# Gate and up products in seven half-width products, output products placed between them, and another order of the recurrent blocks

## The chip, the cores and the metric

The kernel runs on one core of a Trainium2 chip. The number to judge is the device time of one execution in microseconds (us). Five engines of the core appear in the profile: PE (TensorE; its weight loads are shown apart as PEld), DVE (VectorE), ACT (ScalarE), POOL (GpSimd) and SP (SyncE, which here only issues transfers). The engines run side by side, and each works through its own instructions in a fixed order.

## The reference, cut to what matters

Two models follow each other on one sequence of 512 tokens with 1024 features, all in float32. The first has two recurrent blocks (attention, a linear recurrence and a convolution side by side). The second has two layers, each with a mixer, a cross attention and a gated feed-forward part:

```
D_FF = 2816

def swiglu(h, w_gate_up, w_down):
    g, u = jnp.split(h @ w_gate_up, 2, axis=-1)
    return (jax.nn.silu(g) * u) @ w_down

    for l in range(DEPTH):                       # first_block, DEPTH = 2
        h = rms_norm(x, norm_g[l])
        proj = h @ w_in[l]
        ...
    for i in range(DEPTH):                       # second_block
        ...
        x = x + swiglu(rms_norm_2(x, g_ffn[i]), w_gate_up[i], w_down[i])
    return rms_norm_2(x, g_final)
```

## The kernel before, in words

Everything is kept feature-major: `X` is eight tiles of 128 features x 512 tokens. A float32 number is split into a rounded high part and a low part (`hl`, `split`), and each product of two numbers is made of three matmuls (`mm3`): high x high, high x low, low x high.

Weights come in chunks of eight 128x128 blocks (512 KB) in the order in which they are used (`weights`). For a chunk SP issues a load into `wr`, ACT casts it to the high part `wh`, and DVE (or POOL, below) subtracts to get the low part `wl`. `wr`, `wh` and `wl` share six buffers of one pool tag `w`, taken in turn, so that two chunks are in flight. `dense_tile` makes one output tile of 128 features x 512 tokens in one PSUM bank: for eight blocks that is 24 matmuls of 512 columns.

The feed-forward part (`ffn`) has 22 tiles of hidden features, in four groups of 6, 6, 5 and 5 (`FG`). A hidden tile takes two dense tiles, gate and up, from one chunk each; DVE and ACT make silu(gate) x up from them, and `hl` splits the result. The output products of a group (`dn`, eight tiles, each followed by an addition to `X` on DVE) come after the gate and up products of the next group. The last group's output products follow at the end, in the first layer under the next stage's settings, in the second in `finish`, which works in halves of 256 tokens: the same three matmuls with 256 columns.

The recurrent blocks (`block1`, run twice) mix generators, each yielding after a step, in the order of two hand-written strings. In them U is the recurrence's input, G the convolution's input, K the compressed keys, Z, N and C the output gates, Q, V, M and A the attention, B and O the recurrence's tail, T the convolution's tail; V holds the products `vg` with the tokens as output rows (lines L478 to L480). A digit sets `wp`: of every four chunks so many have their low part made on POOL in place of DVE.

Tile decides the order of instructions on each engine from the program's order and the priorities that the code gives.

## Time and profile before

| what | value |
|---|---|
| median of 3 runs | 2249.3 us (2245.65 to 2253.51) |
| the profiled execution, its own time | 2249.68 us |
| its span, first to last instruction | 2247.9 us |
| first recurrent block, second | 0 to 402 us, 402 to 806 us |
| first feed-forward part, second | 1132 to 1490 us, 1857 to 2214 us |
| the last halves (`finish`) | 2214 to 2248 us |
| mean granted clock of PE | 0.986 |

The time of an execution holds a little more than the span. An engine's busy time is the union of its instructions; PE's matmuls overlap each other in it, so that a full row of PE says that it always had a matmul in flight, and the distance from one matmul's start to the next one's says how fast it goes.

### The profile page before, as it was taken

How to read it: one execution, taken by the hardware profiler on the slowest of the kernel's cores; microseconds unless marked ns; L12 is line 12 of the kernel's file. 1: busy time of each engine (PE TensorE's matmuls, PEld its weight loads, DVE VectorE, ACT ScalarE, POOL GpSimd, SP SyncE). 2: the span in 40 equal slices, each digit the busy share in tenths (PEclk: the TensorE clock that was granted, in tenths of full speed). 3: DMA queues.
4: the chain of work that ended last, by engine and by line, in shares of the span. 5: the costliest groups of instructions: out<-in, count | busy, mean ns of one | idle time of the engine just before them, and what ended most of it. 6: DMA issues, size and time to landing. Idle time of an engine off the chain costs nothing. (4 is left out here: it accounts for less than half of the span.)

```text
span 2247.9 us, 29297 instructions
## 1 busy us (share of the span) xinstructions
PE 2149.0 (96%) x11068; PEld 1717.2 (76%) x11068; DVE 1454.2 (65%) x2511; ACT 956.8 (43%) x1821; POOL 390.1 (17%) x419
## 2 busy tenths in 40 slices
PE   8999989999999999998999999999999999999998
PEld 6777867777786778666878888878767788888887
DVE  7998685599877646875565444554776556544444
ACT  4432475334247543664543222233586554322223
POOL 4533201453231151002020000010010202000002
PEclk9999999999999999999999999999999999999999
DMA  4343211233331123212333333322322233333332
GB/s 143 109 121 108 66 29 48 85 108 108 110 97 38 38 75 93 72 43 63 98 105 100 94 94 95 102 85 85 97 60 76 66 85 96 102 94 94 94 101 87
DMA packets 61436, 194.73 MB, mean 87 GB/s; under 512 B 8432, under 2 KB 10480, under 8 KB 61296
## 3 DMA queue, kind: packets, MB, share of 16 engines
q1 hardware_dynamic: 52848, 179.75, 26.9%
q10 hardware_dynamic: 8448, 13.12, 2.1%
q8 instruction: 87, 1.43, 0.3%
q14 instruction: 53, 0.43, 0.1%
HBM read 182.61 MB, written 2.10 MB: 82 GB/s over the span
## 5 line engine op out<-in xcount | busy, mean ns | idle before, releaser
L440 ACT CAST wh<-wr 128x1024 fp32r<-128x1024 f32 (+2 forms) x312 | 322.9, 1035 | 608.0 <-DMA wr<-ws 551.2
L373 DVE TENSOR_TENSOR wl<-wr,wh 128x1024 fp32r<-128x1024 f32 x240 | 297.6, 1240 | 333.1 <-PE ps_m L419 159.5
L418 PE MATMUL ps_m<-xh,wh 128*128 128x512 f32 x808 | 321.8, 398 | 13.0 <-ACT wh L440 8.5
L420 PE MATMUL ps_m<-xh,wl 128*128 128x512 f32 x808 | 319.0, 395 | 1.2 <-POOL wl L373 1.0
L419 PE MATMUL ps_m<-xl,wh 128*128 128x512 f32 x808 | 318.3, 394 | 1.7 <-DVE xl L376 1.7
L420 PE MATMUL ps_s<-xh,wl 128*128 128x512 f32 x680 | 269.7, 397 | 9.8 <-DVE wl L373 6.9
L418 PE MATMUL ps_s<-xh,wh 128*128 128x512 f32 x680 | 269.2, 396 | 2.9 <-ACT ti L385 2.2
L419 PE MATMUL ps_s<-xl,wh 128*128 128x512 f32 x680 | 267.5, 393 | 0.0
L370 POOL TENSOR_TENSOR sq<-sq 128x512 f32<-128x512 f32 (+1 forms) x56 | 78.8, 1406 | 969.0 <-ACT sq L385 969.0
L373 POOL TENSOR_TENSOR wl<-wr,wh 128x1024 fp32r<-128x1024 f32 (+2 forms) x72 | 170.9, 2373 | 403.4 <-PE ps_m L420 152.0
L418 PEld LDWEIGHTS ps_m<-xh,wh 128*128 128x128 f32 x808 | 153.0, 189 | 51.0 <-ACT wh L440 11.2
L385 ACT ACTIVATE p<-ps_s,mn 128x512 f32<-128x512 f32 (+3 forms) x288 | 165.9, 581 | 57.7 <-PE ps_t L819 21.6
L420 PEld LDWEIGHTS ps_m<-xh,wl 128*128 128x128 f32 x808 | 152.7, 189 | 34.6 <-POOL wl L373 1.7
L419 PEld LDWEIGHTS ps_m<-xl,wh 128*128 128x128 f32 x808 | 152.9, 189 | 34.2 <-DVE xl L376 3.5
L376 DVE SCALAR_TENSOR_TENSOR ps_s<-up,params,ps_s 128x512 f32<-128x512 f32 x232 | 169.7, 748 | 2.4
L826 ACT COPY ptt<-ps_t 128x512 f32<-128x512 f32 (+3 forms) x288 | 131.1, 478 | 90.8 <-PE ps_t L819 78.1
L420 PEld LDWEIGHTS ps_s<-xh,wl 128*128 128x128 f32 x680 | 129.2, 190 | 41.8 <-DVE wl L373 9.4
L418 PEld LDWEIGHTS ps_s<-xh,wh 128*128 128x128 f32 x680 | 129.4, 190 | 31.8 <-ACT ti L385 3.8
L419 PEld LDWEIGHTS ps_s<-xl,wh 128*128 128x128 f32 x680 | 129.4, 190 | 27.0
L819 PE MATMUL ps_t<-consts,p 128*128 128x128 f32 x848 | 132.8, 280 | 12.1 <-ACT ptt L826 9.6
L819 PEld LDWEIGHTS ps_t<-consts,p 128*128 128x128 f32 x848 | 97.0, 140 | 53.3 <-ACT ptt L826 24.3
L370 DVE TENSOR_TENSOR X<-ps_m,X 128x512 f32<-128x512 f32 (+1 forms) x100 | 66.4, 664 | 62.0 <-PE ps_m L420 62.0
(518 smaller groups left out, 4090.1 us busy)
## 6 DMA issues: line engine op xcount, KB each, us to landing
wr<-ws SPq DMA_DIRECT2D x318, 512.0 KB, 3.6
strip<-strips ACTq DMA_DIRECT2D x8, 480.0 KB, 3.8
wr<-ws SPq DMA_DIRECT2D x8, 384.0 KB, 3.1
X<-x SPq DMA_DIRECT2D x8, 256.0 KB, 4.9
mem<-mem SPq DMA_DIRECT2D x8, 256.0 KB, 2.7
wr<-ws SPq DMA_DIRECT2D x7, 256.0 KB, 2.8
tab<-tables SPq DMA_DIRECT2D x6, 256.0 KB, 2.7
out_dram<-ox SPq DMA_DIRECT2D x8, 128.0 KB, 1.7
```

The costliest lines, as they stand in the source:

```text
L370: (eng or self.nc.vector).tensor_tensor(out=out, in0=a, in1=b, op=ALU.add)
L373: (eng or self.nc.vector).tensor_tensor(out=out, in0=a, in1=b, op=ALU.subtract)
L376: self.nc.vector.scalar_tensor_tensor(out=out, in0=a, scalar=s, in1=b, op0=op0, op1=op1)
L385: return self.nc.scalar.activation(out, in_, func, **k)
L418: mm(out, ah, bh, start=first, stop=False)
L419: mm(out, ah, bl, start=False, stop=False)
L420: return mm(out, al, bh, start=False, stop=last)
L440: nc.scalar.copy(wh[:, :n], wr[:, :n])
L819: nc.tensor.transpose(t[:, j * P:(j + 1) * P], p[:, j * P:(j + 1) * P], self.con("ident"))
L826: nc.scalar.copy(dst, src)
```

## The change

A hidden tile is now of kind `p` (as before) or `s`. A string, `FFN_ORDER`, gives the kinds of the 22 tiles, 5 `p` and 17 `s`, and puts 24 letters `d` between them, each one output tile of the oldest group that is waiting. For a tile `s` the pair gate and up, the two halves of the input features (even and odd tiles of `X`) and the two halves of the tokens are taken as 2x2 blocks, and the product is made with seven products of blocks and some sums in place of eight products. Each of the seven is a sum over four pairs of input tiles, of three matmuls each with 256 columns: 84 matmuls of 256 in place of 48 of 512. The sums of weights (`ws7`: `s1` to `s4`) and their splitting are made for each tile on DVE and ACT; the sums of inputs (`halves_combined`) once for each layer; the sums of products when they leave PSUM. The raw weights and their sums lie in the six buffers of the tag `pt`, the four split parts (`wah`, `wal`, `wsh`, `wsl`) in the six of `w`. Four PSUM banks, one of each of the tags m, s, t and o, are taken by a tile `s`; there are two of each.

In the recurrent blocks the letters stand in another order, the digit before the first letters is 4 in place of 3, and the 3 that began the second string ends it.

```diff
@@ -29,6 +29,8 @@
 CONV_K = 31
 CPB = 8
 FG = (6, 6, 5, 5)
+FFN_ORDER = "pppspssddsssddssddddsdsdsddddssddddpdssdsddsdd"
+KINDS = [c for c in FFN_ORDER if c in "ps"]
 
 A_ = np.arange
 
@@ -127,8 +129,14 @@
         dense(f"xo{l}", "w_xo_2", (l,), [_r(P * n, P) for n in range(8)], kt(4))
         f0 = 0
         for g, n in enumerate(FG):
-            dense(f"gu{l}{g}", "w_gate_up_2", (l,),
-                  [_r(o + P * (f0 + i), P) for i in range(n) for o in (0, FF)], kt(8))
+            for i in range(f0, f0 + n):
+                gc, uc = _r(P * i, P), _r(FF + P * i, P)
+                if KINDS[i] == "p":
+                    dense(f"gu{l}_{i}", "w_gate_up_2", (l,), [gc, uc], kt(8))
+                    continue
+                ph[f"gu{l}_{i}"] = [
+                    _blk("w_gate_up_2", (l,), _r(P * (4 * c + 2 * q + k), P), cols)
+                    for c in range(2) for k, cols in ((0, gc), (1, gc), (1, uc), (0, uc)) for q in range(2)]
             dense(f"dn{l}{g}", "w_down_2", (l,), [_r(P * m, P) for m in range(8)],
                   [_r(P * (f0 + i), P) for i in range(n)])
             f0 += n
@@ -855,8 +863,8 @@
         return done
 
 
-    FIRST = "/UUG3cUp/GGUKGkGKZZgkZGZkB/kQ|/AkOOkGkGkO/NOAAQkQAQVM"
-    SECOND = "3NTMTATACAMAAAACCCNTQTN|TQATTTMT|TATAA/ATA"
+    FIRST = "/UU4cGUpGGUKGkGKZZ/gZGkZkBkQ|AkOOkGGOk/NOAAQkkQAQVM"
+    SECOND = "NTQTATACA/NAMAACCCTTNTATQA/TTM|MATAATATTA3"
 
     def block1(self, l):
         xhl = self.norm(f"norm_g{l}")
@@ -1553,29 +1561,134 @@
         self.run_held()
         self.residual(f"xo{l}", ys)
 
+    def gate_up(self, name, xhl, _):
+        w = self.weights(name)
+        pg = self.dense_tile(w, xhl)
+        z, th, u = (self.f("d", nm) for nm in ("fg", "ft", "fu"))
+        self.stt(z, pg, 0.5, self.RB)
+        self.act(th, z, AF.Tanh)
+        self.stt(z, th, 1.0, z, op0=ALU.add)
+        pu = self.dense_tile(w, xhl)
+        self.mul(u, pu, self.RB)
+        self.mul(z, z, u)
+        return z, u
+
+    def halves_combined(self, gname):
+
+        h = T // 2
+        slots = iter([("c", T)] * 4 + [("p", T)] * 6 + [("up", 544)] * 3 + [("lup", 516)] + [("tab", T)] * 2)
+        bufs = dict(self.SLOTS, up=3, lup=1, tab=2)
+        out = []
+        for q in range(KD // 2):
+            x1, x2 = self.X[2 * q], self.X[2 * q + 1]
+            g1, g2 = self.par(gname, 2 * q), self.par(gname, 2 * q + 1)
+            ta, tb = self.f("n", "ta"), self.f("n", "tb")
+            self.sub(ta[:, :h], x1[:, h:], x1[:, :h])
+            self.act(ta[:, :h], ta[:, :h], AF.Copy, scale=g1)
+            self.stt(ta[:, h:], x2[:, h:], g2, ta[:, :h], op1=ALU.subtract)
+            self.act(tb[:, :h], x1[:, h:], AF.Copy, scale=g1)
+            self.stt(tb[:, :h], x2[:, h:], g2, tb[:, :h], op1=ALU.subtract)
+            self.stt(tb[:, h:], x2[:, :h], g2, ta[:, h:], op1=ALU.subtract)
+            ts = []
+            for t in (ta, tb):
+                parts = []
+                for nm in ("th", "tl"):
+                    tag, n = next(slots)
+                    parts.append(self.sp.tile([P, n], F32R, name=nm, tag=tag, bufs=bufs[tag])[:, :T])
+                self.split(*parts, t)
+                ts += [tuple(x[:, e * h:e * h + h] for x in parts) for e in range(2)]
+            out.append(ts)
+        return out
+
+    def gate_up7(self, name, xhl, ts):
+
+
+        nc, h, q = self.nc, T // 2, 2 * P
+        px, py, pz, pv = (self.ps(t) for t in "msto")
+        p1, p2, p3, p4, p5, p7, p6 = px[:, :h], px[:, h:], py[:, :h], py[:, h:], pz[:, :h], pz[:, h:], pv[:, :h]
+        ends = (p2, p3, p7, p6)
+        begun = {}
+
+        def product(out, bank, w, o, b, first, last):
+            a = tuple(x[:, o:o + P] for x in w)
+            if first and bank in begun:
+                with self.tc.issue_after(begun[bank].ins):
+                    self.mm3(out, a, b, False, last)
+            else:
+                m = nc.tensor.matmul(out, a[0], b[0], start=first, stop=False)
+                if first:
+                    begun[bank] = m
+                nc.tensor.matmul(out, a[0], b[1], start=False, stop=False)
+                nc.tensor.matmul(out, a[1], b[0], start=False, stop=last)
+
+        for c in range(2):
+            self.nchunk += 1
+            with self.tc.high_priority(offset=self.WPRI):
+                wr, sm = (self.pt(nm, [P, CPB * P], F32) for nm in ("wr7", "ws7"))
+                nc.sync.dma_start(out=wr, in_=self.ap["ws"][CHUNK0[name] + c])
+                wah, wal, wsh, wsl = (self.sp.tile([P, CPB * P], F32R, name=nm, tag="w", bufs=self.NW["w"])
+                                      for nm in ("wah", "wal", "wsh", "wsl"))
+                a11, a12, a22, a21 = (wr[:, k * q:k * q + q] for k in range(4))
+                s1, s2, s3, s4 = (sm[:, k * q:k * q + q] for k in range(4))
+                nc.scalar.copy(wah[:, :3 * q], wr[:, :3 * q])
+                self.sub(wal[:, :3 * q], wr[:, :3 * q], wah[:, :3 * q].bitcast(F32))
+                self.add(s1, a21, a22)
+                self.sub(s2, s1, a11)
+                self.sub(s3, a11, a21)
+                self.sub(s4, a12, s2)
+                nc.scalar.copy(wsh, sm)
+                self.sub(wsl, sm, wsh.bitcast(F32))
+            for w, todo in (((wah, wal), ((p1, 0, 0), (p2, 0, 1), (p4, 1, 2))),
+                            ((wsh, wsl), ((p3, 1, 3), (p5, 2, 0), (p6, 3, 1), (p7, 2, 2)))):
+                for e in range(2):
+                    k = 2 * c + e
+                    x1, x2 = xhl[2 * k], xhl[2 * k + 1]
+                    t1, t2, t3, t4 = ts[k]
+                    lo, hi = (lambda x: tuple(y[:, :h] for y in x)), (lambda x: tuple(y[:, h:] for y in x))
+                    rhs = (lo(x1), lo(x2), t4) if w[0] is wah else (hi(x2), t1, t2, t3)
+                    for (out, bank, o), b in zip(todo, rhs):
+                        product(out, bank, w, o * q + e * P, b, k == 0, k == KD // 2 - 1 and out in ends)
+        s, u34 = self.f("n", "u2"), self.f("n", "u34")
+        z, th, u = (self.f("d", nm) for nm in ("fg", "ft", "fu"))
+        nc.scalar.copy(s[:, :h], p1)
+        self.add(z[:, :h], p2, s[:, :h])
+        self.add(s[:, h:], p6, s[:, :h])
+        pair = lambda x: x.rearrange("p (a n) -> p a n", a=2)
+        self.add(pair(u34), pair(pz), s[:, h:].unsqueeze(1).to_broadcast([P, 2, h]))
+        self.add(z[:, h:], p3, u34[:, :h])
+        self.stt(z, z, 0.5, self.RB)
+        self.act(th, z, AF.Tanh)
+        self.add(u[:, :h], p4, u34[:, h:])
+        self.add(u[:, h:], p5, u34[:, h:])
+        self.mul(u, u, self.RB)
+        self.stt(z, th, 1.0, z, op0=ALU.add)
+        self.mul(z, z, u)
+        return z, u
+
     def ffn(self, l, out=None):
         xhl = self.norm(f"g_ffn_2{l}")
         hid = [None] * len(FG)
 
-        def gu(g):
-            w = self.weights(f"gu{l}{g}")
-            hs = []
-            for i in range(FG[g]):
-                pg = self.dense_tile(w, xhl)
-                z, th, u = (self.f("d", nm) for nm in ("fg", "ft", "fu"))
-                self.stt(z, pg, 0.5, self.RB)
-                self.act(th, z, AF.Tanh)
-                self.stt(z, th, 1.0, z, op0=ALU.add)
-                pu = self.dense_tile(w, xhl)
-                self.mul(u, pu, self.RB)
-                self.mul(z, z, u)
-                hs.append(self.hl("a" if i % 2 else "z", z, "hid"))
-            hid[g] = hs
-
-        gu(0)
-        for g in range(1, len(FG)):
-            gu(g)
-            self.residual(f"dn{l}{g - 1}", hid[g - 1])
+        ts = []
+        todo, n = [], 0
+        for ch in FFN_ORDER:
+            if ch == "d":
+                if todo and next(todo[0], "end") == "end":
+                    todo.pop(0)
+                continue
+            if ch == "s" and not ts:
+                ts += self.halves_combined(f"g_ffn_2{l}")
+            g = next(g for g in range(len(FG)) if n < sum(FG[:g + 1]))
+            z, u = (self.gate_up if ch == "p" else self.gate_up7)(f"gu{l}_{n}", xhl, ts)
+            if hid[g] is None:
+                hid[g] = []
+            hid[g].append(self.hl("a" if len(hid[g]) % 2 else "z", z, "hid"))
+            n += 1
+            if n == sum(FG[:g + 1]) and g < len(FG) - 1:
+                todo.append(self.residual_tiles(f"dn{l}{g}", hid[g]))
+        for t in todo:
+            for _ in t:
+                pass
         name = f"dn{l}{len(FG) - 1}"
         if out is None:
             self.enter("c")
```

The lines of the changed kernel's helpers are numbered 8 higher than before (L418 to L420 of `mm3` are L426 to L428, L373 is L381); L1618 to L1622 are the three matmuls in `product`.

The order of instructions shows what moves where. On PE, in the middle of the first feed-forward part (`ps_` with a letter is the PSUM tile by its tag, `xh` and `xl` the split input, `wh` and `wl` a chunk's split weights), before:

```order
L418 MATMUL ps_s_11208<-xh_10502,wh_11211 128x512
L419 MATMUL ps_s_11208<-xl_10503,wh_11211 128x512
L420 MATMUL ps_s_11208<-xh_10502,wl_11212 128x512
L418 MATMUL ps_s_11208<-xh_10506,wh_11211 128x512
L419 MATMUL ps_s_11208<-xl_10507,wh_11211 128x512
L420 MATMUL ps_s_11208<-xh_10506,wl_11212 128x512
```

and in a tile `s` of the changed kernel (`th` and `tl` are the split sums of inputs, `wsh` and `wsl` those of weights):

```order
L1618 MATMUL ps_s_11181<-xh_10494,wsh_11189 128x256
L1621 MATMUL ps_s_11181<-xl_10495,wsh_11189 128x256
L1622 MATMUL ps_s_11181<-xh_10494,wsl_11190 128x256
L1618 MATMUL ps_t_11182<-th_10788,wsh_11189 128x256
L1621 MATMUL ps_t_11182<-tl_10789,wsh_11189 128x256
L1622 MATMUL ps_t_11182<-th_10788,wsl_11190 128x256
L1618 MATMUL ps_o_11183<-th_10788,wsh_11189 128x256
L1621 MATMUL ps_o_11183<-tl_10789,wsh_11189 128x256
L1622 MATMUL ps_o_11183<-th_10788,wsl_11190 128x256
```

Every matmul has half as many columns and its own weights, and the products of three banks alternate.

On DVE, in the first feed-forward part (`fg` and `fu` are the gate and up tile on their way to the hidden tile, `rb` the norm's factor), the whole work of one hidden tile before:

```order
L373 TENSOR_TENSOR wl_11064<-wr_11061,wh_11063 128x1024
L376 SCALAR_TENSOR_TENSOR fg_11017<-ps_s_10986,rb_10566 128x512
L376 SCALAR_TENSOR_TENSOR fg_11017<-ft_11018,fg_11017 128x512
L373 TENSOR_TENSOR wl_11101<-wr_11098,wh_11100 128x1024
L367 TENSOR_TENSOR fu_11019<-ps_m_11023,rb_10566 128x512
L367 TENSOR_TENSOR fg_11017<-fg_11017,fu_11019 128x512
L373 TENSOR_TENSOR hidl_11057<-fg_11017,hidh_11056 128x512
```

and twelve of the 21 kinds of row that a tile `s` has, where tiles `s` follow each other:

```order
L378 TENSOR_TENSOR u34_11490<-ps_t_11373,u2_11489 128x512
L381 TENSOR_TENSOR wsl_11520<-ws7_11515,wsh_11519 128x1024
L378 TENSOR_TENSOR fg_11491<-ps_s_11372,u34_11490 128x256
L378 TENSOR_TENSOR ws7_11711<-wr7_11710 128x256
L381 TENSOR_TENSOR ws7_11711<-wr7_11710 128x256
L384 SCALAR_TENSOR_TENSOR fg_11491<-fg_11491,rb_10566 128x512
L381 TENSOR_TENSOR wal_11575<-wr7_11571,wah_11574 128x768
L381 TENSOR_TENSOR ws7_11711<-ws7_11711,wr7_11710 128x256
L378 TENSOR_TENSOR fu_11493<-ps_s_11372,u34_11490 128x256
L378 TENSOR_TENSOR fu_11493<-ps_t_11373,u34_11490 128x256
L384 SCALAR_TENSOR_TENSOR fg_11491<-ft_11492,fg_11491 128x512
L381 TENSOR_TENSOR ws7_11711<-wr7_11710,ws7_11711 128x256
```

The rows of one tile's results are mixed with the weights of the tiles behind it: `wsl_11520` belongs to the next tile, `ws7_11711` to the one after it.

On POOL, around the products `vg` of the first recurrent block (`qo` is a query tile's rotation), before:

```order
L370 TENSOR_TENSOR qo_1580<-qo_1580,rs__1582 128x512
L373 TENSOR_TENSOR wl_1771<-wr_1768,wh_1770 128x768
L370 TENSOR_TENSOR qo_1625<-qo_1625,rs__1627 128x512
L373 TENSOR_TENSOR wl_1801<-wr_1798,wh_1800 128x768
L370 TENSOR_TENSOR qo_1717<-qo_1717,rs__1719 128x512
L373 TENSOR_TENSOR wl_1831<-wr_1828,wh_1830 128x768
L373 TENSOR_TENSOR wl_2191<-wr_2188,wh_2190 128x1024
```

and in the changed kernel:

```order
L378 TENSOR_TENSOR qo_1608<-qo_1608,rs__1610 128x512
L381 TENSOR_TENSOR wl_1741<-wr_1738,wh_1740 128x768
L381 TENSOR_TENSOR wl_1771<-wr_1768,wh_1770 128x768
L381 TENSOR_TENSOR wl_1801<-wr_1798,wh_1800 128x768
L378 TENSOR_TENSOR qo_1717<-qo_1717,rs__1719 128x512
L381 TENSOR_TENSOR wl_1831<-wr_1828,wh_1830 128x768
L381 TENSOR_TENSOR wl_1972<-wr_1969,wh_1971 128x1024
```

All four chunks of `vg` are on POOL now, where the first of them (`wl_1741`) was on DVE before. Over the whole program POOL makes 98 low parts in place of 72.

## Rows read from the trace of the kernel before

**Rows 1.** The page's first part: busy time, share of the span, instructions.

```profile
PE 2149.0 (96%) x11068; PEld 1717.2 (76%) x11068; DVE 1454.2 (65%) x2511; ACT 956.8 (43%) x1821; POOL 390.1 (17%) x419
```

**Rows 2.** Busy time by stage: both recurrent blocks, then both feed-forward parts.

```profile
core 0: us, PE busy (x) PEld busy (x) DVE busy (x) ACT busy (x) POOL busy (x), PEclk, DMA share, GB/s
0.00:402.00 402.00, 372.05 (x1971) 292.66 (x1972) 319.69 (x639) 179.52 (x370) 129.38 (x114) 0.98 0.30 89
402.00:806.00 404.00, 380.99 (x2036) 299.96 (x2035) 313.22 (x597) 175.46 (x366) 124.81 (x90) 0.98 0.28 83
1132.00:1490.00 358.00, 355.59 (x1559) 291.37 (x1558) 182.59 (x218) 106.13 (x128) 14.57 (x18) 1.00 0.32 96
1857.00:2214.00 357.00, 356.96 (x1600) 294.29 (x1599) 185.62 (x222) 108.66 (x132) 14.81 (x19) 1.00 0.34 99
```

**Rows 3.** PE's waits in the first feed-forward part: total us, times, longest.

```profile
PE ps_s L418 <- DVE X L370: 2.2, 1, 2.2
PE ps_s L420 <- DVE wl L373: 0.2, 1, 0.2
```

**Rows 4.** Timeline of PE, second feed-forward part: a bank's first matmul (start, duration).

```profile
2030.97 0.40 PE L418 MATMUL ps_m<-hidh,wh 128*128 128x512 f32 x1
...
2035.19 0.39 PE L418 MATMUL ps_s<-xh,wh 128*128 128x512 f32 x1
...
2040.65 0.39 PE L418 MATMUL ps_m<-xh,wh 128*128 128x512 f32 x1
...
2046.09 0.39 PE L418 MATMUL ps_s<-xh,wh 128*128 128x512 f32 x1
```

**Rows 5.** Timeline of PE in `finish`: matmuls of 256 columns, 15 to a bank.

```profile
2214.77 0.28 PE L418 MATMUL ps_s<-hidh,wh 128*128 128x256 f32 x1
...
2220.05 0.28 PE L418 MATMUL ps_m<-hidh,wkh 128*128 128x256 f32 x1
...
2221.37 0.28 PE L420 MATMUL ps_m<-hidh,wkl 128*128 128x256 f32 x1
```

**Rows 6.** Groups of PEld in `finish`, 2214 to 2225: count, busy, mean ns.

```profile
L418 PEld LDWEIGHTS ps_s<-hidh,wh 128*128 128x128 f32 x10 | 1.9, 188 | 0.0
```

**Rows 7.** Groups of DVE by shape: feed-forward part 1200 to 1400, then 256-wide, whole run.

```profile
L373 DVE TENSOR_TENSOR wl<-wr,wh 128x1024 fp32r<-128x1024 f32 x37 | 45.3, 1225 | 70.1 <-PE ps_m L419 35.0 <-PE ps_s L419 31.6 <-ACT wh L440 3.5
L373 DVE TENSOR_TENSOR hidl<-fg,hidh 128x512 fp32r<-128x512 f32 x13 | 9.0, 693 | 11.1 <-ACT hidh L403 11.1
...
L370 DVE TENSOR_TENSOR X<-ps_m,X 128x256 f32<-128x256 f32 x8 | 3.4, 424 | 5.1 <-PE ps_m L420 5.1
```

**Rows 8.** Timeline of DVE, first feed-forward part: rows that follow each other directly.

```profile
1265.08 1.23 DVE L373 TENSOR_TENSOR wl<-wr,wh 128x1024 fp32r<-128x1024 f32 x1 [2.22 <-PE ps_m L419]
1266.22 0.68 DVE L367 TENSOR_TENSOR fu<-ps_m,rb 128x512 f32<-128x512 f32 x1
1266.94 0.69 DVE L367 TENSOR_TENSOR fg<-fg,fu 128x512 f32<-128x512 f32 x1
```

**Rows 9.** Groups of ACT by shape: feed-forward part 1200 to 1400, then `finish`.

```profile
L440 ACT CAST wh<-wr 128x1024 fp32r<-128x1024 f32 x36 | 37.8, 1050 | 83.1 <-DMA wr<-ws 83.1
L403 ACT CAST hidh<-fg 128x512 fp32r<-128x512 f32 x13 | 8.1, 620 | 33.2 <-DVE fg L367 27.4 <-PE ps_m L419 5.8
...
L548 ACT COPY rb<-ps_o 128x256 f32<-128x256 f32 x2 | 0.7, 372 | 5.9 <-PE ps_o L530 5.9
```

**Rows 10.** The page's sixth part: transfers, KB each, us to landing.

```profile
wr<-ws SPq DMA_DIRECT2D x318, 512.0 KB, 3.6
```

**Rows 11.** Timeline of PE in `vg`, first recurrent block: two waits for POOL.

```profile
224.56 0.40 PE L479 MATMUL ps_s<-wl,xh 128*128 128x280 f32 x1 [1.18 <-POOL wl L373]
...
229.23 0.40 PE L479 MATMUL ps_s<-wl,xh 128*128 128x280 f32 x1 [1.32 <-POOL wl L373]
```

**Rows 12.** Groups by shape in both recurrent blocks, POOL then DVE.

```profile
L373 POOL TENSOR_TENSOR wl<-wr,wh 128x1024 fp32r<-128x1024 f32 x63 | 154.1, 2446 | 388.6 <-PE ps_m L420 152.0 <-PE ps_m L419 118.1 <-ACT wh L440 52.9
...
L373 DVE TENSOR_TENSOR ql<-qo,qh 128x512 fp32r<-128x512 f32 x8 | 11.3, 1412 | 4.0 <-ACT qh L403 4.0
```

## The prediction, made before the changed kernel had run

> **What bounds the kernel now.** I read the page first, then each stage, since the page's shares are averages. PE is busy for 96% of the span, DVE for 65% [rows 1]. By stage [rows 2] the two feed-forward parts are the purest case: PE is busy in 355.6 of 358 us and in 357.0 of 357, at a full granted clock, with DVE at 183 and 186. The waits of PE in the first of them come to 2.4 us [rows 3]. So a microsecond of matmul taken out of this stage is a microsecond of the whole, as long as the other engines keep up. The recurrent blocks are different: PE is busy for 372 of 402 us and 381 of 404, DVE for 320 and 313.
>
> A busy PE does not say how fast it goes, so I read the distance between starts. A gate or up tile is 24 matmuls: from 2040.65 to 2046.09, or 0.2267 us each. An output tile of a group of six is 18: from 2030.97 to 2035.19, 0.2344 us each [rows 4]. `finish` has the same three matmuls with 256 columns: 45 of them from 2214.77 to 2220.05, 0.1173 us each, and the slowest stretch behind it has 11 from 2220.05 to 2221.37, 0.120 us each [rows 5].
>
> **The change, part by part.** *PE.* A tile `p` costs 48 x 0.2267 = 10.88 us, a tile `s` 84 x 0.1173 = 9.85 us. That is 1.03 us a tile, and with 17 tiles in each of two layers 35.0 us. Bounds: 0.120 us each leaves 0.80 us a tile, 27 us in all. If a half-width matmul on these inputs went at half of 0.2267, 84 x 0.1133 = 9.52 us would save 1.36 us a tile, 46 us. I take 0.1173, since it comes from the same three matmuls with a new weight block each. The output tiles are the same ones in other places.
>
> Half as many columns for each weight load could uncover the load. The trace shows a load of 188 ns [rows 6] with a matmul every 117 ns: loads overlap matmuls and each other there. The Trainium skill says otherwise: its page "TensorE: Matmul & The Clock Gate" (section "The mechanism" of its part on packing) lets a load overlap running matmuls only when the row groups differ, and here all loads use all rows. By that rule a tile `s` would be slower than `p`; the trace disagrees, with 117 ns against 188.
>
> *DVE.* A row of 1024 lasts 1.23 us, of 512 0.69, of 256 0.42 [rows 7]. When rows follow each other directly the next starts before the end: 1.14 us after a 1024 (1265.08 to 1266.22), but 0.72 us after a 512 whose result it needs (1266.22 to 1266.94) [rows 8]. So I count 1.14, 0.61 and 0.34 us, 0.08 to 0.09 less than the duration, and 0.11 more where a row needs the one ahead of it. For 768, which only crowded stretches show, I interpolate 0.87. A chunk of `s` is then 0.87 + 4 x 0.34 + 1.14 = 3.37 us, two chunks 6.7. The results take five rows of 256 and six of 512 (the low part of the hidden tile among them), 5.4 us. With about five direct successions, 0.6, a tile `s` needs 12.7 us of DVE. A tile `p` needs 2 x 1.14 + 5 x 0.61, 5.4 us with one succession. A letter `d` needs 0.61 and its share of a weight chunk: 1.47 us for six inputs, 1.32 for five, where PE takes 4.22 or 3.52.
>
> The sums over the string: PE 17 x 9.85 + 5 x 10.88 + 16 x 4.22 + 8 x 3.52 = 317.5 us. DVE 17 x 12.7 + 5 x 5.4 + 16 x 1.47 + 8 x 1.32 = 277 us, with the sums of inputs (4 x (4 x 0.34 + 2 x 0.61) = 10.3) and the norm's eight low parts (4.9) 292 us, 92% of PE's. DVE goes from half busy to nearly full, and what was cover becomes the thing to look at.
>
> So I split the string. Behind the first `ppp` come `spssddsssddss`: PE 8 x 9.85 + 10.88 + 4 x 4.22 = 106.6 us, DVE 8 x 12.7 + 5.4 + 4 x 1.47 = 112.9 us. DVE is short by 6.3 us. The rest, `ddddsdsdsddddssddddpdssdsddsdd`, has PE 178 us (12 letters d of six inputs, 8 of five) against DVE 148, so nothing is lost there. How far can DVE be ahead? The `wsh` of the next chunk takes the buffer that this chunk's `wah` frees half-way, and is used one chunk later, 42 x 0.1173 = 4.9 us. ACT's cast (1.05 us [rows 9]) and DVE's 1.23 come out of that, so the lead is at most 2.6 us. Short by 6.3, less 2.6 of lead, with 1 to 3 us for rows that stand in DVE's queue waiting for ACT: I take 6 us of waiting for each layer, 12 in all. Bounds: 0 if the order hides it, 19 for each layer if the rows never overlap (the second rival).
>
> *What stays covered.* ACT casts for a tile `s` at most 4 x 1.05 us, copies one 256 (0.37) and makes a tanh and a high part of 512 (0.62 each): under 6 us of 9.85 [rows 9]. Uncovered it would cost as the chain below does. Each tile still loads two chunks of 512 KB, 3.6 us each from issue to landing [rows 10], so even one after the other they take 7.2 of 9.85 us; and the raw chunks lie in `pt`, three chunks deep.
>
> *The recurrent blocks.* POOL makes 26 more low parts, 13 in each block, and DVE 26 fewer: 26 x 1.14 = 30 us off an engine that is 79% busy and on whose account PE waits little. For POOL it is 26 x 2.45 = 64 us [rows 12] on 254 of 806 busy. In `vg` PE waited 1.18 and 1.32 us for POOL's low parts, with only 3.4 us of work between (224.56 to 229.23 less the wait) [rows 11]; one chunk of each block joins them. The letters move steps past each other on all queues, and the trace prices none of that. Bounds: PE idles 30 and 23 us in the two blocks, of which 6.9 is the start, so no order can give more than some 45; if each of the 26 moved chunks made PE wait 1.3 us, 34 us would be lost. I take 2 us of gain, near nothing, since few waits of PE end with a DVE row.
>
> *The sum*, against the profiled execution's own 2249.7 us, which stands 0.4 above the median: 2249.7 - 35.0 + 12 - 2 = 2224.7, so **2225 us**.
>
> **The rivals.** *Half-width matmuls go faster* than in `finish`, at half of 0.2267: 46 us saved, with 8 us of waits and the 2 us of the blocks 2249.7 - 46 + 8 - 2 = 2210 us. For it: the inputs are mostly the same `xh` and `xl` that go at 0.2267 where `hidh` goes at 0.2344. Against: the sums lie in other buffers.
>
> *DVE becomes the bound.* If each of the 21 rows of a tile needs the one ahead of it, a tile `s` is 12.1 + 21 x 0.11 = 14.4 us. The stretch of thirteen letters then needs 8 x 14.4 + 5.4 + 5.9 = 126.5 us against 106.6; less the lead of 2.6 and with 2 us for ACT, 19 us are lost for each layer: 2249.7 - 35 + 38 - 2 = 2251 us, no change. For it: DVE works in order and many rows wait for ACT. Against: rows of different tiles are mixed, so that few need the one ahead.
>
> *The slower side: the buffers' chain.* Each half chunk waits for a buffer, then for ACT's cast, then for DVE's subtraction, with 2.6 us to spare. If the order puts more rows than that ahead of `wsl` (four rows of 512 are 2.4 us), PE waits in every chunk. At 35/68 = 0.51 us for each of the 68 chunks the gain is gone; at 1 us the time is 2249.7 - 35 + 68 - 2 = 2281 us. For it: the result rows of a tile are 5.4 us. Against: in the order they are mixed singly between the weights' rows.
>
> *POOL in the recurrent blocks.* Each moved chunk makes PE wait 1.3 us: 2225 + 34 = 2259 us. For it: a DVE row on two operands lasts 1412 ns there, where its like in the feed-forward part lasts 693 [rows 7, 12], so POOL's rows hold DVE up. The page "SBUF — State Buffer" of the Trainium skill (section "SBUF: two separate sides") gives the reason: a DVE instruction with two SBUF inputs and a POOL instruction share a port pair, and one blocks the other for its whole length. By that rule alone the 64 us more of POOL could stop DVE for up to as long; the trace agrees with the blocking.
>
> *Weight loads uncovered.* If no load hid and each matmul took the 188 ns of its load, a tile `s` would be 15.8 us, 4.9 more than `p`, and the time 2249.7 + 34 x 4.9 = 2416 us. This is the page's rule on row groups at work; [rows 5] speak against it.
>
> **How the numbers follow.** The forecast with its waits between 0 and 12 us a layer has 0.60, faster matmuls 0.12, DVE as the bound 0.12, the chain 0.09, POOL 0.05, uncovered loads 0.02. About 0.3%, or 7 us, is what can be told from no change, so faster means under 2242.5. The first two cases are faster; of DVE as the bound I give 0.03 to faster, 0.06 to the same and 0.03 to slower, since it comes in degrees; of POOL 0.02 to faster, 0.03 to slower; the chain mostly (0.05) to slower and 0.04 to the same. Together 0.77, 0.10 and 0.13. The range: 2206 to 2252 leaves out 0.06 below and 0.13 above. The forecast's own is 2213 to 2237.
>
> **What the next profile would show.** Right: starts of 256-wide matmuls 0.117 us apart in both feed-forward parts; DVE near 290 us busy in each; the part from its norm to its last output tile 11 to 17 us shorter; waits of PE on `wsl` or `wal` gathered in the first third, about 6 us a layer. Wrong: distances over 0.13 us; waits for DVE in every chunk; a granted clock under 1.00 in these parts, as where PE waits now; or a recurrent block longer by over 5 us, with waits for POOL.

## The result, and the profile after

The changed kernel takes 2220.4 us (median of 4 runs, 2218.8 to 2221.4) against 2247.5 us for the kernel before, run beside it (4 runs, 2243.1 to 2253.5). The ratio is 0.9875, with a 95% interval of 0.9853 to 0.9897: 28 us, or 1.25%, faster. The forecast was 2225 us, 2206 to 2252. A second measurement, beside the last experiments, gave 2224.4 and 0.9889 (0.9867 to 0.9911).

The page's first part answers to [rows 1]:

```profile
PE 2117.7 (96%) x12292; PEld 1743.1 (79%) x12292; DVE 1685.9 (76%) x3077; ACT 1039.4 (47%) x1955; POOL 453.3 (20%) x445
```

PE's share has not moved; DVE has 232 us more. The same four stages as in [rows 2], between their new bounds (first both recurrent blocks, then both feed-forward parts):

```profile
core 0: us, PE busy (x) PEld busy (x) DVE busy (x) ACT busy (x) POOL busy (x), PEclk, DMA share, GB/s
0.00:396.00 396.00, 370.01 (x1972) 289.13 (x1972) 318.83 (x628) 180.35 (x370) 157.68 (x126) 0.98 0.27 90
396.00:798.00 402.00, 380.95 (x2033) 300.09 (x2033) 305.55 (x583) 175.26 (x365) 158.00 (x104) 0.98 0.26 83
1119.00:1469.00 350.00, 343.07 (x2165) 306.73 (x2164) 302.33 (x509) 146.26 (x195) 14.72 (x18) 1.00 0.29 98
1837.00:2183.00 346.00, 342.98 (x2204) 308.78 (x2203) 301.39 (x510) 148.34 (x198) 15.44 (x19) 1.00 0.30 98
```

In the feed-forward parts DVE goes from 183 and 186 us to 302 and 301. PE is still busy for nearly all of them, but now idles 6.9 us in the first where it idled 2.4. To compare lengths I go from the first `xh` of a feed-forward norm to the first `xh` of the next norm (to the end of the span for the second part, `finish` included): 355.8 to 349.4 us and 390.3 to 380.1, 16.6 us in all.

A half-width stretch on PE's timeline (start, duration), 54 starts from the first row to the last, answers to [rows 4, 5]:

```profile
1225.06 0.28 PE L1618 MATMUL ps_s<-xh,wsh 128*128 128x256 f32 x1
1225.17 0.28 PE L1621 MATMUL ps_s<-xl,wsh 128*128 128x256 f32 x1
...
1231.45 0.28 PE L1618 MATMUL ps_s<-xh,wsh 128*128 128x256 f32 x1
```

That is 0.1183 us each. The loads there still last 0.19 us, so they overlap the matmuls as in `finish`.

PE's waits in the first feed-forward part (total us, times, longest), in place of [rows 3]:

```profile
PE ps_s L428 <- DVE wl L381: 2.0, 2, 1.3
PE ps_s L426 <- ACT wh L448: 1.6, 1, 1.6
PE ps_m L426 <- ACT wh L448: 1.0, 1, 1.0
PE ps_s L426 <- DVE X L378: 0.9, 1, 0.9
PE ps_m L1618 <- ACT wah L1633: 0.5, 1, 0.5
PE ps_m L428 <- DVE wl L381: 0.5, 1, 0.5
```

No row names `wsl` or `wal`. The two `wl` rows lie at 1120 to 1135 us, before the first tile `s`; 0.2 us of such waits stood there before, 2.5 stand there now. DVE's timeline ahead of the first of them:

```profile
1118.57 0.41 DVE L378 TENSOR_TENSOR ws<-wr 128x256 f32<-128x256 f32 x1
1118.90 0.42 DVE L381 TENSOR_TENSOR ws<-wr 128x256 f32<-128x256 f32 x1
1119.24 1.22 DVE L381 TENSOR_TENSOR wl<-wr,wh 128x1024 fp32r<-128x1024 f32 x1
```

Twelve rows of sums for the first tiles `s` are run that early, from 1109 to 1133 us, and stand ahead of the low parts that PE needs first. In every kernel below that makes these sums once on DVE the waits are 2.5 us, with the sums made twice 4.7, with the sums on POOL 1.5, and without a tile `s` 0.2 to 0.6: these waits come from the sums.

What is new in the middle is `wh`, the cast weights of an output tile. The timeline of all engines around the longest, with the row of SP's queue that issues the load:

```profile
1308.77 0.33 SPq L442 DMA_DIRECT2D wr<-ws  x1
...
1313.54 0.28 PE L1622 MATMUL ps_t<-th,wsl 128*128 128x256 f32 x1
1314.29 1.05 ACT L448 CAST wh<-wr 128x1024 fp32r<-128x1024 f32 x1 [3.19 <-DMA wr<-ws]
...
1315.38 0.50 PE L426 MATMUL ps_s<-hidh,wh 128*128 128x512 f32 x1 [1.57 <-ACT wh L448]
```

PE runs out of half-width work at 1313.8. The raw weights of the next output chunk were asked for only at 1308.77 and landed 5.5 us later; ACT had been idle 3.19 us for them. An output chunk's raw weights `wr` are loaded into a buffer of the ring `w` (six buffers taken in turn), in which every chunk's high and low parts lie too; those of an `s` chunk go to `pt` and are there early. What SP waited for before that load, and the packets that still moved in the load's last 2.7 us:

```profile
SPq L442 <- PE ps_t L1621: 2.0, 1, 2.0
```

```profile
DMA packets 10, 0.03 MB, mean 12 GB/s; under 512 B 2, under 2 KB 2, under 8 KB 10
```

SP stood 2.0 us until a matmul of the tile `s` was done with its buffer: the load is late. It is also slow: with the 3.6 us of [rows 10] and a cast of 1.05 us the weights would have been ready at 1313.4, before PE needed them. Ten packets of 0.03 MB came last; why, no run shows. Right behind this wait of 1.57 us the granted clock is 0.50 (1.2 of 2.4 GHz) for 3.4 us:

```profile
1316.40:1319.80 3.40, 3.40 (x10) 2.72 (x10) 3.40 (x7) 1.14 (x2) 0.00 (x0) 0.50 0.18 39
```

The first third, `spssddsssddss`, from its first `s` at 1168.6 to the `dddd` at 1276.9, is where the waits were forecast. Its window, and two of DVE's groups in it:

```profile
1168.60:1276.90 108.30, 107.97 (x792) 101.95 (x791) 100.73 (x184) 45.71 (x59) 0.00 (x0) 1.00 0.32 107
```

```profile
L381 DVE TENSOR_TENSOR wsl<-ws,wsh 128x1024 fp32r<-128x1024 f32 x15 | 18.4, 1223 | 1.6 <-ACT wsh L1639 1.5
L378 DVE TENSOR_TENSOR u<-ps_o,u 128x256 f32<-128x256 f32 x7 | 2.9, 421 | 0.2
```

PE idles 0.33 us. DVE is busy 100.7 us where I had counted 112.9: nearly full, and not late. Eight tiles `s` have sixteen rows `wsl` and eight rows `u<-ps_o`. Fifteen and seven lie here: the first low parts are made ahead of the third, and the results of its last tile under the `dddd` behind it.

### The profile page after: what moved, and what is told of

The parts are those of the page before. It is cut to its first block, busy times and chain, and to the rows that moved or that the text cites. A ratio compares the mean times of both kernels' runs of the same rounds, so it can differ in the third digit from the quotient of the medians.

```text
span 2217.0 us, 32569 instructions
## 1 busy us (share of the span) xinstructions
PE 2117.7 (96%) x12292; PEld 1743.1 (79%) x12292; DVE 1685.9 (76%) x3077; ACT 1039.4 (47%) x1955; POOL 453.3 (20%) x445
## 3 DMA queue, kind: packets, MB, share of 16 engines
q1 hardware_dynamic: 52848, 179.75, 24.5%
## 5 line engine op out<-in xcount | busy, mean ns | idle before, releaser
L448 ACT CAST wh<-wr 128x1024 fp32r<-128x1024 f32 (+2 forms) x244 | 251.9, 1032 | 389.6 <-DMA wr<-ws 297.8
L381 POOL TENSOR_TENSOR wl<-wr,wh 128x1024 fp32r<-128x1024 f32 (+2 forms) x98 | 235.3, 2401 | 399.6 <-PE ps_m L427 250.9
L381 DVE TENSOR_TENSOR wl<-wr,wh 128x1024 fp32r<-128x1024 f32 (+1 forms) x146 | 185.0, 1267 | 118.8 <-PE ps_m L427 45.3
L426 PE MATMUL ps_m<-xh,wh 128*128 128x512 f32 x536 | 215.6, 403 | 8.7 <-ACT wh L448 6.7
L428 PE MATMUL ps_m<-xh,wl 128*128 128x512 f32 x536 | 213.5, 398 | 2.9 <-POOL wl L381 1.6
L427 PE MATMUL ps_m<-xl,wh 128*128 128x512 f32 x536 | 211.5, 395 | 2.5 <-DVE xl L384 2.5
L428 PE MATMUL ps_s<-xh,wl 128*128 128x512 f32 x408 | 165.4, 405 | 15.4 <-POOL wl L381 7.8
L426 PE MATMUL ps_s<-xh,wh 128*128 128x512 f32 x408 | 163.6, 401 | 2.4 <-ACT wh L448 2.3
L427 PE MATMUL ps_s<-xl,wh 128*128 128x512 f32 x408 | 162.7, 399 | 0.0
L426 PEld LDWEIGHTS ps_m<-xh,wh 128*128 128x128 f32 x536 | 101.6, 190 | 34.3 <-ACT wh L448 6.9
L428 PEld LDWEIGHTS ps_m<-xh,wl 128*128 128x128 f32 x536 | 101.5, 189 | 27.3 <-POOL wl L381 3.3
L1639 ACT CAST wsh<-ws 128x1024 fp32r<-128x1024 f32 x68 | 71.6, 1053 | 93.7 <-PE ps_t L1621 41.1
L428 PEld LDWEIGHTS ps_s<-xh,wl 128*128 128x128 f32 x408 | 79.0, 194 | 38.9 <-POOL wl L381 12.1
L388 DVE TENSOR_SCALAR p<-p,sc 128x512 f32<-128x512 f32 (+3 forms) x272 | 101.5, 429 | 2.4
```

What stands on the lines that cost most here:

```text
L381: (eng or self.nc.vector).tensor_tensor(out=out, in0=a, in1=b, op=ALU.subtract)
L388: self.nc.vector.tensor_scalar(out=out, in0=a, scalar1=s1, scalar2=None, op0=op0)
L426: mm(out, ah, bh, start=first, stop=False)
L427: mm(out, ah, bl, start=False, stop=False)
L428: return mm(out, al, bh, start=False, stop=last)
L448: nc.scalar.copy(wh[:, :n], wr[:, :n])
```

## The experiments

Each kernel was timed against the kernel before on the same chip, whose median was 2247.9 to 2250.6.

**The two halves of the change apart.** The first kernel has the old strings, the second is the kernel before with the new ones:

```diff
-    FIRST = "/UU4cGUpGGUKGkGKZZ/gZGkZkBkQ|AkOOkGGOk/NOAAQkkQAQVM"
-    SECOND = "NTQTATACA/NAMAACCCTTNTATQA/TTM|MATAATATTA3"
+    FIRST = "/UUG3cUp/GGUKGkGKZZgkZGZkB/kQ|/AkOOkGkGkO/NOAAQkQAQVM"
+    SECOND = "3NTMTATACAMAAAACCCNTQTN|TQATTTMT|TATAA/ATA"
```

> The changed kernel with the old strings FIRST and SECOND, so that only the feed-forward part is changed. Theory A (the prediction's terms: 35.0 us of matmuls less 12 us of waiting in the feed-forward parts, 2 us in the recurrent blocks): 23 us under the kernel before, so 2 us above the changed kernel, near 2224. Theory B (the stage lengths of the two traces: the feed-forward parts shrank by 6.4 and 10.2 us, the recurrent blocks by 6.3 and 1.4, the stretches between by the rest): 17 us under the kernel before, so about 10 us above the changed kernel, near 2231.

> The kernel before with the new strings FIRST and SECOND alone. Theory A: the reordering is worth 2 us, 2245 to 2246. Theory B: it is worth 8 us in the blocks, and what follows them may add a few, 2236 to 2240. A third reading: the new order was made for the feed-forward part that follows it and does nothing alone, 2247 to 2249.

The feed-forward part alone: 2223.7 us, 0.9883 (0.9869 to 0.9898), so 23 to 30 us gained. The blocks alone: 2247.4 us, 0.9989 (0.9978 to 1.0000), 0 to 5 us. The first agrees with theory A. The second rules theory B out, but cannot tell A's 2 us from no gain at all. The two gains, 1.17% and 0.11%, add up to 1.28% where the whole is 1.25%. One execution of a stage is not an exact measure of it. The first recurrent block is the same program in the changed kernel and in the next one below; its window there and there:

```profile
4.00:396.00 392.00, 370.01 (x1972) 289.13 (x1972) 318.83 (x628) 179.07 (x369) 156.30 (x112) 0.98 0.27 90
155.00:162.00 7.00, 6.40 (x28) 5.18 (x28) 6.89 (x11) 1.19 (x2) 2.46 (x2) 1.00 0.46 142
```

```profile
4.00:404.00 400.00, 374.32 (x1972) 292.65 (x1972) 314.34 (x627) 178.43 (x369) 155.65 (x112) 0.97 0.29 88
155.00:162.00 7.00, 6.02 (x14) 4.76 (x15) 6.89 (x10) 1.36 (x2) 2.54 (x1) 0.51 0.25 75
```

The same 1972 matmuls take 392 and 400 us. From 155 to 162 one execution has the full clock and does 28 of them, the other has 0.51 and does 14; such stretches fall in other places in each execution. In twelve profiles of this same block, from its first `xh` to the next norm's, it took 391.5 to 399.7 us.

**Only the order, no half-width product.**

```diff
-FFN_ORDER = "pppspssddsssddssddddsdsdsddddssddddpdssdsddsdd"
+FFN_ORDER = "pppppppddpppddppddddpdpdpddddppddddpdppdpddpdd"
```

> The changed kernel with every gate and up tile of the kind p, so the new order of the output tiles and of the blocks without any half-width product. Theory A: the 35 us and the 12 us of waiting both belong to the s tiles, so this stands 23 us above the changed kernel, near 2244. Theory B: the waits that the trace shows in the feed-forward parts, 10 and 5 us, come where output tiles follow gate and up tiles and load their raw weights late; with the p tiles DVE has more room but the buffers of the ring w are fuller, so part of these waits may stay: then the time is near 2244 to 2250, and the waits before output tiles are seen in the profile.

2257.5 us, 1.0040 (1.0028 to 1.0053), above both theories. The new order by itself costs some 10 us (2257.5 against 2247.4 with the same blocks), and the tiles `s` then bring 2257.5 - 2220.4 = 37 us. PE's waits in the first feed-forward part, and what DVE waited for at one of them:

```profile
PE ps_s L428 <- DVE wl L381: 2.3, 4, 0.7
PE ps_s L426 <- DVE X L378: 2.1, 1, 2.1
PE ps_m L428 <- DVE wl L381: 1.6, 3, 0.7
```

```profile
1233.02 1.22 DVE L381 TENSOR_TENSOR wl<-wr,wh 128x1024 fp32r<-128x1024 f32 x1 [4.60 <-PE ps_s L427]
```

DVE, busy for half of this stage, sat idle 4.60 us until PE's matmul on an older `wh` was done, and only then could write `wl`: a buffer of the ring `w` was missing, not DVE's time.

**The raw weights of output chunks out of the ring `w`.** All three groups first, then the second and third alone:

```diff
-                wr = w("wr", F32, "w")
+                wr = self.pt("wrd", [P, CPB * P], F32) if name[:2] == "dn" and name[-1] != "3" else w("wr", F32, "w")
```

```diff
-                wr = w("wr", F32, "w")
+                wr = self.pt("wrd", [P, CPB * P], F32) if name[:2] == "dn" and name[-1] in "12" else w("wr", F32, "w")
```

> The changed kernel with the raw weights of the output tiles that stand between the gate and up tiles loaded into the ring pt, where the raw weights of the s tiles are loaded too, and not into the ring w, where they wait for a buffer. If the late load is what makes TensorE wait at the steps from s to d (about 10 us in the first feed-forward part, 5 in the second): those waits go and the time falls by 5 to 12 us, to 2208 to 2215. If DVE's load is the cause, as the prediction had it: the waits stay, within 3 us of the changed kernel. A third way: pt is only three chunks deep, so the s tiles' own loads come later and the kernel gets slower.

2216.7 us, 0.9862 (0.9848 to 0.9875). Less than hoped. The waits at 1313 and 1418 are gone, and another has come, which the waits of PE and the timelines of SP's queue and of DVE show:

```profile
PE ps_s L428 <- DVE wsl L381: 3.3, 2, 2.6
```

```profile
1233.81 0.33 SPq L442 DMA_DIRECT2D wrd<-ws  x1
1236.88 8.68 SPq L1628 DMA_DIRECT2D wr<-ws  x2
```

```profile
1242.38 0.43 DVE L378 TENSOR_TENSOR ws<-wr 128x256 f32<-128x256 f32 x1 [2.60 <-DMA wr<-ws]
```

The output chunk asked for at 1233.81 took a place in `pt`; the `s` chunk behind it could be asked for only at 1236.88, and DVE stood 2.60 us for it. So the first group should stay where it was:

> The changed kernel with the raw weights of the second and third group of output tiles alone in the ring pt; those of the first group stay in the ring w. With all three in pt the waits on ACT's wh from 1300 us on were gone, but 2.6 us of waiting on DVE's wsl came in the first third, where SP held the loads of two s chunks back. If both readings hold, the first feed-forward part has neither: 344 to 346 us in place of 349.4, the second 1 to 2 us less, and the time 2212 to 2216. If the late load was not the cause, the time stays at 2220; if pt makes the later s chunks late as well, waits on wsl come behind 1300 us and nothing is gained.

2210.4 us, 0.9836 (0.9811 to 0.9860): 37 us under the kernel before and, by the two ratios of the changed kernel (0.9875 and 0.9889), 9 to 12 us under that. Its feed-forward parts are 343.6 and 377.0 us, in place of 349.4 and 380.1. PE's waits in the first:

```profile
PE ps_s L428 <- DVE wl L381: 2.0, 2, 1.3
PE ps_s L426 <- DVE X L378: 0.9, 1, 0.9
PE ps_m L428 <- DVE wl L381: 0.5, 1, 0.5
PE ps_s L426 <- ACT wh L448: 0.3, 1, 0.3
```

Of the changed kernel's rows those at the stage's two ends are left, and 0.3 us on `wh`. In the second part the rows `wh` and `wah`, 1.0 and 0.5 us in the changed kernel, are gone. The changed kernel's second profile (below) has such rows too, 1.3 us in the first part and 2.0 in the second. So the ring `w` as the cause of the waits at the output tiles is shown by this. The size of the gain is less certain. The interval of this kernel (up to 0.9860) touches the first of the changed kernel's two (from 0.9853) and just misses the second (from 0.9867), on different chips. In the two stages 8.9 us are seen against the first profile and 5.6 against the second.

**How near DVE is to its bound.** The sums of every chunk made twice, which leaves the result as it is:

```diff
-                self.add(s1, a21, a22)
...
+                for _ in range(2):
+                    self.add(s1, a21, a22)
...
```

> The changed kernel with the four rows of 256 that make the sums of a weight chunk repeated once, the second time with the same operands and result, so DVE has 4 x 0.34 = 1.4 us more for each chunk, 2.7 us for a tile s, 46 us a layer, and nothing is changed for the other engines. Theory A (the prediction: DVE needs 12.7 us for a tile s in a first third that has 106.6 us for eight of them, and is the reason for the waits): that third is short by 22 us more in each layer, the later letters still have cover: about 40 us slower than the changed kernel, 2260. Theory B (the waits are those for a buffer of the ring w, and DVE has room): less than 15 us slower, 2223 to 2235.

2266.8 us, 1.0087 (1.0060 to 1.0114), 46 us slower than the changed kernel. Here A was near, and B far off. The window around the first third, then PE's waits in the whole part:

```profile
1177.00:1298.00 121.00, 113.43 (x799) 104.07 (x798) 119.14 (x241) 45.53 (x60) 0.00 (x0) 1.00 0.28 96
```

```profile
PE ps_s L1622 <- DVE wsl L381: 3.1, 2, 1.6
...
PE ps_s L428 <- DVE wsl L381: 1.1, 2, 0.9
...
PE ps_m L1622 <- DVE wal L381: 0.7, 1, 0.7
```

DVE is busy 119 of 121 us, and now the rows `wsl` and `wal` stand there. From its first `s` to `dddd` this third takes 118.9 us (1179.8 to 1298.7) against 108.3. The whole part takes 371.4 us against 349.4, and of these 22 us 4.7 lie ahead of the first `s`, 10.6 in the third and 6.7 behind it; A had put all 22 into the third. So the bound that the prediction saw is real, and the changed kernel lies just under it.

**More tiles `s`, on the better kernel.** Two more a layer, then four:

```diff
-FFN_ORDER = "pppspssddsssddssddddsdsdsddddssddddpdssdsddsdd"
+FFN_ORDER = "pppssssddsssddssddddsdsdsddddssddddsdssdsddsdd"
```

```diff
-FFN_ORDER = "pppspssddsssddssddddsdsdsddddssddddpdssdsddsdd"
+FFN_ORDER = "pssssssddsssddssddddsdsdsddddssddddsdssdsddsdd"
```

> The kernel with the raw weights of the second and third output group in pt, and in each layer two more tiles p made as s: the one p in the first third and the one p in the last. The price per tile, 10.88 - 84 x 0.1185 = 0.93 us, gives 3.7 us for four tiles: 2206 to 2207 if DVE still has cover for its 7.3 us more a tile. With the sums made twice, half of the time that DVE was given came back as waiting of TensorE; if that holds here, 4 x 7.3 / 2 = 15 us are lost and 3.7 won: 2221.

> As the kernel with two more tiles s in each layer, and the second and third tile of the feed-forward part made s as well, so 21 of 22 tiles a layer are s. By the price per tile 7.4 us under 2210, 2203, if DVE has cover. If DVE is near its bound in the first third, as the sums made twice suggest, there are now eleven tiles s with 12.7 us of DVE each against 9.95 of TensorE and two output tiles between them: 11 x 2.75 less the 5.6 that the two output tiles give back, some 22 us a layer are lost, and the time is 2245 or more.

2219.6 us, 0.9863 (0.9841 to 0.9885), and 2251.7 us, 1.0013 (0.9998 to 1.0028). Neither gains on 0.9836 with none added (the first interval overlaps that one's), though each tile takes 0.93 us from PE. Both come near the expectation that has DVE near its bound (2221, and 2245 or more). With four more, PE's longest rows in the first part are these:

```profile
PE ps_m L1622 <- DVE wal L381: 6.7, 7, 1.9
PE ps_o L538 <- POOL rs L375: 4.7, 1, 4.7
```

**Half-width products only behind the first third.**

```diff
-FFN_ORDER = "pppspssddsssddssddddsdsdsddddssddddpdssdsddsdd"
+FFN_ORDER = "pppppppddpppddppddddsdsdsddddssddddpdssdsddsdd"
```

> The changed kernel with the first eight of the seventeen tiles s made as p, in the same order, so there are half-width products only behind the first third. Theory A (the first third is bound by DVE, which takes back 6 us a layer of the 8.2 that its eight tiles save): only 2.2 us a layer is lost, so 2220 + 4 = 2224 to 2225. Theory B (the trace shows no waits in the first third, so its tiles bring their full 1.03 us): 16.5 us are lost, 2237, and a few more if the waits for DVE's wl that the kernel of all p showed between its first output tiles (three of 0.86 us a layer) come back: up to 2242.

2244.9 us, 0.9993 (0.9978 to 1.0008). (The sums of the inputs are made at the first `s`, here from rows `X` to which output tiles have been added already, so this kernel computes another sum; the work is the same.) Sixteen tiles made `p` cost 24 us, 1.5 each, above even B; in the lengths of the two parts it is 20 to 23. A is out: the tiles of the first third had brought their gain. What goes beyond 16 x 0.94 = 15 us is seen in part: the tiles `p` in this order wait as in the kernel of all `p`, and PE's `wl` rows are 2.7 and 1.8 us here, 2.0 and 0.5 in the changed kernel.

**What halving costs.** In the kernel of all `p`, each product in two halves:

```diff
-        pg = self.dense_tile(w, xhl)
+        pg = self.half_tile(w, xhl)
...
+            for e in range(2):
+                sl = slice(e * h, e * h + h)
...
+                    last = self.mm3(o, a, bb, False, e == 1 and k == len(rhs) - 1)
```

> The kernel of all tiles p, in the new order, but with each of their 512-wide matmuls made as two of 256 columns on the same weight block, one half after the other, so each tile has 96 matmuls in place of 48 and loads its weights twice. Nothing else changes. If a half-width matmul costs 0.118 where half of a 512-wide one is 0.1135, this is 96 x 0.0045 = 0.43 us a tile and 19 us for 44 tiles over the kernel of all p: 2257.5 + 19 = 2276. If halving is free, 2257; if some loads of 188 ns are not covered when a weight comes again after three matmuls, over 2300.

2284.5 us, 1.0166 (1.0138 to 1.0193), 27 us over the kernel of all `p` where 19 were expected. From PE's timeline, 13 starts apart:

```profile
1141.82 0.28 PE L427 MATMUL ps_m<-xl,wh 128*128 128x256 f32 x1
...
1143.38 0.28 PE L428 MATMUL ps_m<-xh,wl 128*128 128x256 f32 x1
```

0.120 us, where half of 0.2267 is 0.1133. The difference, 0.0067 x 96 x 44 tiles, is 28 us, which is all of it. So the price of a 256-wide matmul lies in the width, not in which inputs it has, and the rival "half-width matmuls go faster" is out.

**The sums on POOL.**

```diff
-                self.add(s1, a21, a22)
+                self.add(s1, a21, a22, nc.gpsimd)
...
```

> The changed kernel with the four rows of 256 that make the sums of each chunk on POOL, so DVE has 2.7 us less for each tile s, 46 us a layer, and POOL, idle there, has them. If DVE's load is what the waits of the changed kernel come from, up to 17 us of waiting go: 2203 to 2215. If the waits come from late loads, the time stays at 2218 to 2222. If POOL's rows, which are slower (2446 against 1225 ns for 1024 columns), make the sums late, or hold DVE's two-operand rows up as the slower DVE rows beside POOL in the recurrent blocks suggest, the time is over 2235, with waits on wsl or wsh in every tile.

2227.5 us, 0.9902 (0.9878 to 0.9926): 3 us slower than the changed kernel beside it, which is within what can be told: no gain, and not the loss of a chain either, so in none of the three ranges. The groups of the first feed-forward part by shape, POOL's sums as minimum/median/maximum in ns, then DVE's rows (busy us, mean ns):

```profile
L381 POOL TENSOR_TENSOR ws<-wr x31: 725/1197/4446, 1173.6 to 1432.0; 128x256 f32<-128x256 f32 x31
```

```profile
L375 DVE TENSOR_TENSOR fu<-fu,rb 128x512 f32<-128x512 f32 x17 | 16.5, 969 | 0.0
L378 DVE TENSOR_TENSOR fg<-ps_s,u 128x256 f32<-128x256 f32 x17 | 7.1, 418 | 0.3
```

The same DVE row `fu<-fu,rb` lasts 688 ns in the changed kernel. A DVE row with two operands in SBUF grows by 281 ns, one with an operand in PSUM (`ps_s`, 419 before) does not, and POOL's row of 256 lasts from 0.7 up to 4.4 us. So part of what DVE is relieved of comes back as longer rows.

The changed kernel once more, beside the last three:

> The changed kernel itself, unaltered, beside the variants on one chip: 2220 expected from the first measurement. With the kernel that keeps the raw weights of the second and third output group in pt at 2210, the difference of 10 us should be seen again as a ratio near 0.9875 here against 0.983 to 0.984 for its variants.

2224.4 us, 0.9889 (0.9867 to 0.9911). Its feed-forward parts are 345.7 and 380.5 us; the first has only 0.8 us of waiting on `wh` and no half clock. Of the 349.4 us of the first profile some 4 were chance.

## Why the prediction was right, and where it was not

**PE's saving** was 35.0 us by 0.1173 and a tile `p` of 10.88 us. At the measured 0.1183 a tile `s` is 9.94 us, 34 tiles save 32.0. The term was 3 us too large, inside its bounds of 27 to 46. The tiles against their own order gave 37 timed and 29 to 33 in the lengths of the two parts. The uncovered weight load, the rival at 2416 us, did not come: loads of 0.19 us, 0.118 us apart. The rule of the Trainium skill's page "TensorE: Matmul & The Clock Gate" (section "The mechanism"), by which a load overlaps running matmuls only when the row groups differ, is not borne out by these rows. The same section of the Trainium skill also lets a load into the background weight buffer go ahead; these rows do not speak against that, and no run shows that buffer apart.

**The waits** were to be 12 us, all in the first third and for DVE. Their size was near, their place was wrong, and their cause was right for less than half. I sum the distances between PE's starts over both parts, as far as each is more than 0.05 us beyond 0.118 us (256 columns), 0.227 (`p`) or 0.234 (`d`): 3.3 us before, 19.0 in the first profile of the changed kernel, 15.6 in the second. So 12 to 16 are new. Some 5 of them lie at the start of the parts, where DVE's low parts stand behind the sums, a place that I had not priced. Another 5 to 9 lie at output tiles whose raw weights came late, the stretch at half clock with them, a step that I gave nothing ("covered", with the 3.6 us of a transfer): the ring `w` lets the load be asked for some 5 us ahead of need, and transfers of 5.0 and 5.5 us did not make it. Each first third has 1.3 us in place of 6.

The step that failed is the count of DVE for that third, 112.9 us, of which it was to be short by 6.3: it is 100.7 measured, in 108.3. The rows were sized well. Taking off the 11.3 for one `p` and four `d` leaves 89.4 us, and eight tiles at the 12.1 of their rows, less the 5.4 of the last tile's results and the 2.0 of the low parts made ahead (the forecast's lead of 2.6), are 89.4 too. So two things were wrong: the results of the last tile do not belong to the third, since the four `d` behind it cover them, and the 0.6 a tile for direct successions is not seen. (The second rival counts 21 rows a tile; by the prediction's own list they are 23, which would make it some 2 us a layer slower.) The right sum rests on luck here: waits of another place and, for the most part, another cause came to the same 12.

**DVE as the bound** did not decide, but it was a close rival: 2.7 us more a tile cost 46 us. Two signs of being right were not met: no wait on `wsl` or `wal` in the first third, and parts shorter by 6 to 11 us where 11 to 17 were forecast.

**The recurrent blocks**: 2 us forecast, 0 to 5 measured alone. POOL has 61 us more work there (254 to 316), as forecast with 64. DVE lost 26 rows, by its durations 32 us, but its busy time fell by 8.5 only (632.9 to 624.4); so other rows got longer, and it did not hurt, since POOL's and ACT's rows end most of PE's waits there. The Trainium skill's page "SBUF — State Buffer" (section "SBUF: two separate sides") says that a POOL instruction and a DVE instruction with two SBUF inputs block each other; the rows of the sums on POOL agree, 688 to 969 ns with two SBUF inputs and 419 to 418 with one in PSUM. PE's two waits in `vg` [rows 11] did not grow: 1.2 us in three waits in the first block. Elsewhere they did: PE's waits for POOL's low parts in both blocks are 12.1 us before and 14.8 in the changed kernel, and its waits that end with ACT fell from 24.5 to 16.3. So the rival POOL was right in direction and far too large.

**Open.** The feed-forward part alone was measured at 23 to 30 us. Its two stages in three profiles shrank by 16.6 to 19.9, which is the 32.0 saved less the 12 to 16 of new waits. The rest lies in stages whose code did not change, where single profiles differ by more than that; the runs cannot say whether it is more than chance. So some 3 to 13 us of the timed gain have no cause that is shown, and that 2225 lies so near to 2220 owes something to them.

## What to carry to other kernels

Before an engine is blamed for a wait, ask what it waited for itself: here ACT stood idle for a load at the very moment when PE waited for ACT, and moving two groups of loads to another ring gave 9 to 12 us by the ratios where more of the fast products gave nothing. When the work of a stretch is counted, ask which of it can be done ahead of the stretch and which falls behind it; and look also at where the work done ahead goes, here in front of rows that PE needed first. Count an engine that is over 90% busy as a limit for the next step and not for this one: the same kernel lost 46 us from a few rows more. And take gains from timed pairs, not from the lengths of a stage in two profiles.

## What the runs showed of the hardware that was not expected

A float32r matmul of 256 columns keeps to 0.117 to 0.120 us, whatever the input, and one of 512 to 0.227 (0.234 for the hidden tiles), so each half of a 0.227 costs 5 to 7 ns more than half of it. Loads of 512 KB landed in 3.3 us (median) and now and then in 5.0 to 5.5, and the slowest ended in PE's wait of 1.57 us. Identical stages of one program spread by 8 us in 392, and stretches at half clock come at other places in each execution. POOL's 256-wide row with two SBUF operands went from 0.7 to 4.4 us beside a full DVE.
